# Rotary scores on one core: rows of k laid out like q, whole-batch loads, rotation in place, column order restored by ScalarE

## The chip, the cores and the metric

The kernel runs on one core of one Trainium2 chip. The metric is the device time in microseconds (us). The kernel before takes 808.53 us, the median of three runs (807.85 to 809.18). Everything is fp32.

## The reference

```python
batch, seq, heads, dim = 16, 512, 16, 64
q1, q2 = q[..., :half_dim], q[..., half_dim:]
q_rot = np.concatenate([q1 * cos_q - q2 * sin_q,
                        q1 * sin_q + q2 * cos_q], axis=-1)
# k_rot: the same with k
scores = np.einsum('bshd,bthd->bsht', q_rot, k_rot)
```

Here q and k are [batch, seq, heads, dim], 33.5 MB each, cos and sin are [seq, dim/2], and the scores are [batch, seq, heads, seq], 268.4 MB. There is no scaling and no softmax. For each batch and head the rotated rows of q are multiplied with all 512 rotated rows of k, over a depth of 64.

## The kernel before, in words

**Tiles.** A batch has 512 rows, cut into C = 4 chunks of 128. For q and for the output, chunk c holds the rows 4p + c, with p the partition (line 43 and line 45, pattern "(p c)"). For k, chunk c holds the rows 128c + p (line 44, pattern "(c p)"). One row of q or k is 16 heads x 64 numbers, 4 KB, so a partition's four rows of q lie side by side in memory and its four rows of k do not. One row of the output is 16 heads x 512 numbers, 32 KB.

**One tile of output.** There are 64 tiles, i = 0 to 63, tile i being chunk i mod 4 of batch i // 4. For each, `scores` (line 162) runs eight steps p = 0 to 7. Each step handles two heads: two matmuls into a PSUM buffer `ps` of two banks (three such buffers), then one ScalarE copy of 128x1024 numbers from `ps` to the staging tile `st` (line 179). After the eighth step SyncE issues one store of 4 MB (line 184). There are three staging buffers. Batch 0 is handled in quarters (units of four heads, lines 79 to 87), with stores of 1 MB (line 182), so that work can start early.

**What feeds it.** `load_pair` (line 91) loads two chunks of q or of k, 1 MB, on SyncE's queue. `rope` (line 102) rotates one chunk by three VectorE instructions: a product with cos into a new tile `rot` (line 128), a product with a signed sin table into `part` (line 131), and a sum with the halves of `part` swapped (line 134). `transposed` (line 140) turns a rotated chunk in two groups of four 128x128 transposes on TensorE, each group into one PSUM bank (two such banks), and names the place in `kT` or `qT` where the bank is copied. For k of batches 1 to 15 that place is 128 neighbouring columns for each pair of heads (lines 158 and 159), so a copy of a bank reads and writes in order.

**Order.** It is written out by hand (`tc.manual_schedule()`); each engine works through its own instructions in the order of the program. In tile i of the main loop (lines 247 to 274) the steps 1 and 3 carry the transposes of q of chunk i + 1, copied by VectorE (line 267), and the steps 5 and 6 carry those of k of chunk i + 4, copied by ScalarE (line 269). VectorE's rotation of q for chunk i + 2 and of k for chunk i + 5 is dealt out between them. At the end of each tile one 1 MB load is issued behind the tile's store: of q in odd tiles, of k in even ones. Three input buffers of 1 MB serve k, two serve q.

**Tables.** cos and sin are loaded twice, once in k's row order (runs of 128 bytes) and once in q's (runs of 512 bytes), on ScalarE's queue (line 53), and a signed sin table is built for each (lines 59 and 60).

Of the kernel before, what the change touches and what calls it, by code (L numbers as in the profile page):

```python
# [10 lines left out]
def kernel(  # L11
# [8 lines left out]
    nc = tc.nc  # L20
# [14 lines left out]
    rot_pool = ctx.enter_context(tc.tile_pool(name="rot", bufs=2))  # L35
# [7 lines left out]
    q_v = q.rearrange("b (p c) h d -> b p c h d", c=C)  # L43
    k_v = k.rearrange("b (c p) h d -> b p c h d", c=C)
# [3 lines left out]
    tabs = {}  # L48

    def load_tables(which, pat):  # L50
        for name, src in (("cos", cos), ("sin", sin)):
            t = const_pool.tile([P, C, HD], fp32, name=f"{name}_{which}")
            nc.scalar.dma_start(t, src.rearrange(pat, c=C))
            tabs[name, which] = t

    def build_table(which):

        ss = const_pool.tile([P, C, 2, HD], fp32, name=f"ss_{which}")
        nc.scalar.copy(out=ss[:, :, 0, :], in_=tabs["sin", which])
        nc.scalar.mul(ss[:, :, 1, :], tabs["sin", which], -1.0)  # L60
        tabs["ss", which] = ss.rearrange("p c x j -> p c (x j)")

    in_tiles = {}
    IN_BUFS = {"k": 3, "q": 2}

    def in_tile(which, pair):
        t = in_pool.tile(
            [P, 2, H * D], fp32, tag=which + "_in", bufs=IN_BUFS[which], name=which + "_sb"
        )
        in_tiles[which, pair] = t  # L70
        return t
# [5 lines left out]
    units = {}  # L77

    def load_units(which, head, heads):
        n = C * heads * D  # L80
        t = early[:, load_units.used : load_units.used + n]
        load_units.used += n
        t = t.rearrange("p (c e) -> p c e", c=C)
        src = (k_v if which == "k" else q_v)[0, :, :, head : head + heads, :]
        nc.sync.dma_start(t.rearrange("p c (h d) -> p c h d", d=D), src)
        for h in range(0, heads, G):
            units[which, (head + h) // G] = t[:, :, D * h : D * (h + G)]

    load_units.used = 0

    def load_pair(which, pair):

        b, x = divmod(pair, C // 2)
        if b >= B:
            return
        t = in_tile(which, pair)
        src = (k_v if which == "k" else q_v)[b, :, 2 * x : 2 * x + 2]
        nc.sync.dma_start(t.rearrange("p c (h d) -> p c h d", h=H), src)

    rots = {}  # L100

    def rope(which, n):


        a = rot_pool.tile([P, H * D], fp32, tag="rot_" + which, name=which + "_rot")
        bt = rot_pool.tile([P, H * D], fp32, tag="part", name="part")
        cs, ss = tabs["cos", which], tabs["ss", which]
        if n < C:
            src = units[which, n]
            sv = "p c (g j) -> p c g j"  # L110
            v1 = "p (c g j) -> p c g j"
            k1 = {"c": C, "j": HD}
            cs = cs.unsqueeze(2).to_broadcast((P, C, 2 * G, HD))
            ss = ss.unsqueeze(2).to_broadcast((P, C, G, D))
            k2 = {"c": C, "j": D}
        else:
            src = in_tiles[which, n // 2][:, n % 2]
            sv = "p (g j) -> p g j"
            v1 = "p (g j) -> p g j"
            k1 = {"j": HD}  # L120
            cs = cs[:, n % C].unsqueeze(1).to_broadcast((P, 2 * H, HD))
            ss = ss[:, n % C].unsqueeze(1).to_broadcast((P, H, D))
            k2 = {"j": D}
        swapped = bass.AP(bt.tensor, bt.offset + HD, [bt.ap[0], (D, H), (-HD, 2), (1, HD)])
        a4 = a.rearrange("p (h x j) -> p h x j", x=2, j=HD)
        rots[which, n] = a
        return [
            lambda: nc.vector.tensor_tensor(  # L128
                a.rearrange(v1, **k1), src.rearrange(sv, j=HD), cs, op=mult
            ),  # L130
            lambda: nc.vector.tensor_tensor(  # L131
                bt.rearrange(v1, **k2), src.rearrange(sv, j=D), ss, op=mult
            ),
            lambda: nc.vector.tensor_tensor(a4, a4, swapped, op=add),  # L134
        ]
# [4 lines left out]
    def transposed(which, n, g):  # L140

        rot = rots[which, n]
        bank = ps_t_pool.tile([P, 4, P], fp32, tag="ps_t", name="bank")
        for x in range(4):
            if n < C:
                src = rot.rearrange("p (c e) -> p c e", c=C)[:, x, P * g : P * (g + 1)]
            else:
                src = rot[:, P * (4 * g + x) : P * (4 * g + x + 1)]
            nc.tensor.transpose(bank[:, x, :], src, ident)  # L149
        if which == "q":  # L150
            if n not in qT:
                qT[n] = qt_pool.tile([P, HP, P], fp32, tag="qT", name="qT_t")
            dst = qT[n][:, 4 * g : 4 * g + 4, :]
        else:
            b = n // C
            if b not in kT:
                kT[b] = kt_pool.tile([P, HP, S], fp32, tag="kT", name="kT_t")
            t = kT[b].rearrange("p h (c t) -> p h c t", c=C)
            dst = t[:, 2 * n + g] if n < C else t[:, 4 * g : 4 * g + 4, n % C]
        return bank, dst  # L160

    def scores(i, p, st):

        ps = ps_s_pool.tile([P, 2, S], fp32, tag="ps_s", name="ps")
        b = i // C
        if b == 0:
            c, hp = divmod(p, 2)
            lhs, rhs = qT[i][:, C * hp + c], kT[0][:, 2 * i + hp]
        else:
            lhs, rhs = qT[i][:, p], kT[b][:, p]  # L170
        for r in range(2):
            nc.tensor.matmul(  # L172
                out=ps[:, r, :],
                lhsT=lhs[64 * r : 64 * r + 64, :],
                rhs=rhs[64 * r : 64 * r + 64, :],
                start=True,
                stop=True,
            )
        nc.scalar.copy(out=st[:, 2 * p : 2 * p + 2, :], in_=ps)  # L179
        if b == 0 and p % 2 == 1:  # L180
            c = p // 2
            nc.sync.dma_start(o_v[0, c, :, G * i : G * (i + 1)], st[:, G * c : G * (c + 1)])
        elif b > 0 and p == HP - 1:
            nc.sync.dma_start(o_v[b, i % C], st)

    def tr_act(which, n):
        for g in range(2):
            bank, dst = transposed(which, n, g)
            nc.scalar.copy(out=dst, in_=bank)  # L189

    def run(ops):
        for op in ops:
            op()

    with tc.manual_schedule():
        load_tables("k", "(c p) j -> p c j")
        load_tables("q", "(p c) j -> p c j")
# [3 lines left out]
        load_pair("k", 2)  # L201
        load_pair("q", 2)
        load_pair("k", 3)
        make_identity(nc, ident)
        build_table("k")
        build_table("q")
        run(rope("k", 0))
        tr_act("k", 0)
        run(rope("q", 0))
        tr_act("q", 0)  # L210


        for i in range(C):
            st = st_first[i] if i < 2 else stage_pool.tile([P, H, S], fp32, tag="stage", name="st")
            late = []
            if i > 0:
                late = [("k", C + i - 1, 0), ("k", C + i - 1, 1)]
# [6 lines left out]
            for p in range(HP):  # L224
                scores(i, p, st)
                if p in (0, 1) and late:
                    bank, dst = transposed(*late.pop(0))
                    dve.pop(0)()
                    nc.vector.tensor_copy(out=dst, in_=bank)  # L229
                if i == 0 and p == 1:  # L230
                    load_pair("k", 4)
                if i == 0 and p == 3:
                    load_pair("q", 3)
                if p in (2, 6):
                    m = len(dve) - (6 if p == 2 else 3) + (-3 if i == C - 1 else 0)
                    run(dve[:m])
                    dve = dve[m:]
                    tr_act(*nxt.pop(0))
            run(dve)
            if i == 1:  # L240
                load_pair("k", 5)
            elif i == 3:
                load_pair("q", 4)
                load_pair("k", 6)


        for i in range(C, NST):
# [11 lines left out]
            for p in range(HP):  # L259
                scores(i, p, st)  # L260
                if p not in tr:
                    continue
                bank, dst = transposed(*tr[p])
                if tr[p][0] == "q":
                    run(dve[:1])
                    dve = dve[1:]
                    nc.vector.tensor_copy(out=dst, in_=bank)  # L267
                else:
                    nc.scalar.copy(out=dst, in_=bank)  # L269
            run(dve)  # L270
            if i % 2 == 1:
                load_pair("q", (i + 1) // 2 + 2)
            else:
                load_pair("k", (i + 4) // 2 + 3)
# [30 lines left out]
```

## Time and profile before

| What | Value |
|---|---|
| time, median of three runs | 808.53 us |
| the profiled execution's own time | 811.69 us |
| its span (first to last event in the profile) | 809.9 us |
| busy in the span: TensorE, ScalarE, VectorE | 689.5, 561.8, 522.6 us |
| read from and written to memory by DMA | 67.37 MB and 268.44 MB |
| granted TensorE clock, mean | 0.937 |
| first and last issue of a 4 MB store (line 184) | 71.5 and 787.4 us |

The profile lists, for each engine, how long its instructions were busy, and for each group of instructions (line, operation, tiles, shape) the count, the total and the mean of one. The row of DMA digits is the share of the core's 16 DMA engines that were busy, in 40 slices of the span. A DMA is cut into packets, one for each contiguous run of memory; the trace holds the start, the duration and the size of every packet. "Idle before" is the time in which an engine waited ahead of a group, with what released it.

### The profile page before, as it was taken

To read this page: it belongs to the slowest core of one execution; us is meant where nothing else is said; L and a number is where in the kernel's file an instruction comes from. 1 tells how busy PE (TensorE), PEld (TensorE's weight loads), DVE (VectorE), ACT (ScalarE), POOL (GpSimd) and SP (SyncE) were. 2 spreads that over 40 slices of the span, in tenths; PEclk is the share of its full clock that TensorE was granted. 3 is DMA by queue.
4 is the path that set the end of the run, shared out by engine and by line. 5 is a ranking of instruction groups with operands and counts; after the bars stand their busy time and mean duration, and the time that the engine had idled before them with its cause. 6 is when DMAs were issued, how large, how long until landed. Compare 5 with 4: busy or idle time off the path is not lost.

```text
span 809.9 us, 7719 instructions
## 1 busy us (share of the span) xinstructions
PE 689.5 (85%) x3072; PEld 295.6 (36%) x3072; DVE 522.6 (65%) x508; ACT 561.8 (69%) x649; POOL 0.7 (0%) x6
## 2 busy tenths in 40 slices
PE   4989998898888888888879799797988989889870
PEld 3444443343333333333334333343333333333320
DVE  7899786655767656756568575576755856565400
ACT  4888886676767776767767668676767666777670
POOL 0000000000000000000000000000000000000000
PEclk9999999989999999999999999998989899999895
DMA  9999999999999999999999999999999999999995
GB/s 346 424 424 441 410 420 435 431 419 439 433 420 437 430 423 436 431 424 438 430 422 436 431 424 438 425 429 437 387 431 398 426 410 430 388 367 392 412 415 222
DMA packets 26916, 336.31 MB, mean 415 GB/s; under 512 B 3328, under 2 KB 4608, under 8 KB 13312
## 3 DMA queue, kind: packets, MB, share of 16 engines
q1 hardware_dynamic: 25536, 335.55, 98.2%
q8 instruction: 24, 0.39, 0.2%
q10 hardware_dynamic: 1344, 0.26, 0.2%
q14 instruction: 12, 0.10, 0.0%
HBM read 67.37 MB, written 268.44 MB: 415 GB/s over the span
## 4 chain that ended last, share of the span: by engine, by line
DMA 61%; PE 27%; ACT 6%; DVE 2%; issue 1%; ACTq 0%
DMA out_dram<-st 61%; PE ps L172 20%; PE bank L149 7%; ACT st L179 6%; DVE part L131 1%; DMA cos_k<-in_cos_dram 1%; DVE kT_t L229 0%; DVE q_rot L134 0%; DVE k_rot L134 0%; DVE k_rot L128 0%; DVE q_rot L128 0%; ACTq L300 0%; ACTq L179 0%
## 5 line engine op out<-in xcount | busy, mean ns | idle before, releaser
L179 ACT COPY st<-ps 128x1024 f32<-128x1024 f32 x512 | 494.8, 1019 | 213.5 <-DMA out_dram<-st 145.1
L172 PE MATMUL ps<-kT_t,qT_t 64*128 64x512 f32 x2048 | 546.5, 647 | 82.6 <-ACT st L179 82.6
L172 PEld LDWEIGHTS ps<-kT_t,qT_t 64*128 64x128 f32 x2048 | 180.7, 195 | 277.8 <-ACT st L179 145.5
L128 DVE TENSOR_TENSOR q_rot<-q_sb,cos_q 128x1024 f32<-128x1024 f32 x60 | 73.3, 1221 | 163.4 <-DMA q_sb<-in_q_dram 163.4
L267 DVE COPY qT_t<-bank 128x512 f32<-128x512 f32 x118 | 80.9, 686 | 78.9 <-PE bank L149 78.7
L149 PEld LDWEIGHTS bank<-ident,q_rot 128*128 128x128 f32 x512 | 60.3, 154 | 106.8 <-issue 85.6
L149 PE MATMUL bank<-ident,q_rot 128*128 128x128 f32 x512 | 92.8, 311 | 2.6 <-DVE q_rot L134 2.6
L149 PE MATMUL bank<-ident,k_rot 128*128 128x128 f32 x512 | 83.8, 288 | 11.1 <-DVE k_rot L134 10.8
L149 PEld LDWEIGHTS bank<-ident,k_rot 128*128 128x128 f32 x512 | 54.6, 142 | 104.9 <-issue 52.2
L134 DVE TENSOR_TENSOR k_rot<-k_rot,part 128x1024 f32<-128x1024 f32 x64 | 78.3, 1224 | 2.1
L134 DVE TENSOR_TENSOR q_rot<-q_rot,part 128x1024 f32<-128x1024 f32 x64 | 77.8, 1215 | 0.2
L128 DVE TENSOR_TENSOR k_rot<-k_sb,cos_k 128x1024 f32<-128x1024 f32 x60 | 73.1, 1218 | 0.0
L131 DVE TENSOR_TENSOR part<-k_sb,ss_k 128x1024 f32<-128x1024 f32 x60 | 73.0, 1217 | 0.0
L131 DVE TENSOR_TENSOR part<-q_sb,ss_q 128x1024 f32<-128x1024 f32 x60 | 72.9, 1215 | 0.0
L269 ACT COPY kT_t<-bank 128x512 f32<-128x512 f32 x112 | 66.8, 597 | 0.0
L128 DVE TENSOR_TENSOR k_rot<-early,cos_k 128x1024 f32<-128x1024 f32 x4 | 4.9, 1220 | 5.0 <-DMA cos_k<-in_cos_dram 5.0
L189 ACT COPY qT_t<-bank 128x512 f32<-128x512 f32 x10 | 5.6, 616 | 3.0 <-PE bank L149 3.0
L189 ACT COPY kT_t<-bank 128x512 f32<-128x512 f32 x10 | 5.5, 604 | 2.0 <-PE bank L149 2.0
L229 DVE COPY kT_t<-bank 128x512 f32<-128x512 f32 x6 | 4.1, 686 | 2.6 <-PE bank L149 2.6
L128 DVE TENSOR_TENSOR q_rot<-early,cos_q 128x1024 f32<-128x1024 f32 x4 | 4.9, 1217 | 0.0
L131 DVE TENSOR_TENSOR part<-early,ss_q 128x1024 f32<-128x1024 f32 x4 | 4.9, 1216 | 0.0
L131 DVE TENSOR_TENSOR part<-early,ss_k 128x1024 f32<-128x1024 f32 x4 | 4.9, 1215 | 0.0
(11 smaller groups left out, 3.4 us busy)
## 6 DMA issues: line engine op xcount, KB each, us to landing
out_dram<-st SPq DMA_DIRECT2D x60, 4096.0 KB, 27.7
k_sb<-in_k_dram SPq DMA_DIRECT2D x30, 1024.0 KB, 30.2
q_sb<-in_q_dram SPq DMA_DIRECT2D x30, 1024.0 KB, 28.8
out_dram<-st SPq DMA_DIRECT2D x16, 1024.0 KB, 11.3
early<-in_k_dram SPq DMA_DIRECT2D x1, 1536.0 KB, 9.1
early<-in_q_dram SPq DMA_DIRECT2D x1, 1536.0 KB, 12.4
early<-in_k_dram SPq DMA_DIRECT2D x1, 512.0 KB, 4.0
early<-in_q_dram SPq DMA_DIRECT2D x1, 512.0 KB, 5.5
```

Of the source, the lines that this page charges most:

```text
L128: lambda: nc.vector.tensor_tensor(a.rearrange(v1, **k1), src.rearrange(sv, j=HD), cs, op=mult),
L131: lambda: nc.vector.tensor_tensor(bt.rearrange(v1, **k2), src.rearrange(sv, j=D), ss, op=mult),
L134: lambda: nc.vector.tensor_tensor(a4, a4, swapped, op=add),
L149: nc.tensor.transpose(bank[:, x, :], src, ident)
L172: nc.tensor.matmul(out=ps[:, r, :], lhsT=lhs[64 * r : 64 * r + 64, :], rhs=rhs[64 * r : 64 * r + 64, :], start=True, stop=True,)
L179: nc.scalar.copy(out=st[:, 2 * p : 2 * p + 2, :], in_=ps)
L189: nc.scalar.copy(out=dst, in_=bank)
L229: nc.vector.tensor_copy(out=dst, in_=bank)
L267: nc.vector.tensor_copy(out=dst, in_=bank)
L269: nc.scalar.copy(out=dst, in_=bank)
```

## The change

- k's rows are laid out like q's: partition p holds the rows 4p to 4p + 3 of both. One pair of tables and one signed table serve q and k.
- A load takes a whole batch of q or k, 2 MB, in which each partition reads one run of 16 KB. Before, each load took two chunks, 1 MB, with runs of 8 KB for q and 4 KB for k. There are two buffers of 2 MB each for q and k. In the main loop q of batch b + 2 is issued behind the store of tile 4b + 2 and k of batch b + 3 behind that of tile 4b + 3; the other tiles issue no load.
- The rotation is done in place, in the input tile: the product with sin goes to `part` first (one buffer instead of two), then the input is multiplied by cos in itself, then the sum is made in itself. The tiles `rot` are gone. The transposes read the input tile, which stays occupied until they are done. The two products are one entry of the list that deals out VectorE's work; in batch 0 the sum is two instructions of half the size.
- The columns of `kT` stay in the order (chunk, partition), but column (c, p) now stands for row 4p + c of k. The scores' columns come out in that order, and ScalarE's copy from `ps` to `st` reads PSUM with the innermost step of 128 numbers (four of them, then the next column), which puts the columns back in order. In batch 0 the reordering is done when the bank is copied to `kT`, and the copy of the scores is as before.

```diff
-    k_v = k.rearrange("b (c p) h d -> b p c h d", c=C)
+        "k": k.rearrange("b (p c) h d -> b p c h d", c=C),
...
-    IN_BUFS = {"k": 3, "q": 2}
...
-        t = in_tile(which, pair)
-        src = (k_v if which == "k" else q_v)[b, :, 2 * x : 2 * x + 2]
-        nc.sync.dma_start(t.rearrange("p c (h d) -> p c h d", h=H), src)
+        t = in_pool.tile([P, C, H * D], fp32, tag=which + "_in", name=which + "_sb")
+        batches[which, b] = t
+        nc.sync.dma_start(t.rearrange("p c (h d) -> p c h d", h=H), dram[which][b])
...
+            x4 = x.rearrange("p (h x j) -> p h x j", x=2, j=HD)
+            swapped = bass.AP(part.tensor, part.offset + HD, [part.ap[0], (D, H), (-HD, 2), (1, HD)])
+            adds = [(x4, swapped)]
...
+        def products():
+            nc.vector.tensor_tensor(pv, xs, ss, op=mult)
+            nc.vector.tensor_tensor(xc, xc, cs, op=mult)
+
+        def sums():
+            for y, z in adds:
+                nc.vector.tensor_tensor(y, y, z, op=add)
...
-            t = kT[b].rearrange("p h (c t) -> p h c t", c=C)
-            dst = t[:, 2 * n + g] if n < C else t[:, 4 * g : 4 * g + 4, n % C]
-        return bank, dst
+            if n < C:
+                dst = kT[b][:, 2 * n + g].rearrange("p (t c) -> p t c", c=C)
+                src = bank.rearrange("p c t -> p t c")
+            else:
+                dst = kT[b][:, 4 * g : 4 * g + 4, P * (n % C) : P * (n % C + 1)]
+        copy(out=dst, in_=src)
...
-        nc.scalar.copy(out=st[:, 2 * p : 2 * p + 2, :], in_=ps)
+        so, si = st[:, 2 * p : 2 * p + 2, :], ps
+        if b > 0:
+            so = so.rearrange("s r (t c) -> s r t c", c=C)
+            si = si.rearrange("s r (c t) -> s r t c", c=C)
+        nc.scalar.copy(out=so, in_=si)
...
-        load_tables("k", "(c p) j -> p c j")
-        load_tables("q", "(p c) j -> p c j")
+        for t, src in ((cos_t, cos), (sin_t, sin)):
+            nc.scalar.dma_start(t, src.rearrange("(p c) j -> p c j", c=C))
...
-        load_pair("k", 2)
-        load_pair("q", 2)
-        load_pair("k", 3)
+        load("k", 1)
+        load("q", 1)
...
-                if i == 0 and p == 1:
-                    load_pair("k", 4)
-                if i == 0 and p == 3:
-                    load_pair("q", 3)
+                if p == 3 and i < 2:
+                    load("kq"[i], 2)
...
-            if i == 1:
-                load_pair("k", 5)
-            elif i == 3:
-                load_pair("q", 4)
-                load_pair("k", 6)
+        load("k", 3)
...
-            if i % 2 == 1:
-                load_pair("q", (i + 1) // 2 + 2)
-            else:
-                load_pair("k", (i + 4) // 2 + 3)
+            if i % C == C - 2:
+                load("q", i // C + 2)
+            elif i % C == C - 1:
+                load("k", i // C + 3)
```

More of the change, by code (lines that the diff above doesn't have):

```diff
@@ L34 @@
     in_pool = ctx.enter_context(tc.tile_pool(name="in", bufs=2))
-    rot_pool = ctx.enter_context(tc.tile_pool(name="rot", bufs=2))
+    part_pool = ctx.enter_context(tc.tile_pool(name="part", bufs=1))
     kt_pool = ctx.enter_context(tc.tile_pool(name="kt", bufs=2))
@@ L40 @@
     ps_t_pool = ctx.enter_context(tc.psum_pool(name="ps_t", bufs=2))
-    q_v = q.rearrange("b (p c) h d -> b p c h d", c=C)
-    k_v = k.rearrange("b (c p) h d -> b p c h d", c=C)
+    dram = {
+        "q": q.rearrange("b (p c) h d -> b p c h d", c=C),
+        "k": k.rearrange("b (p c) h d -> b p c h d", c=C),
+    }
     o_v = out.rearrange("b (p c) h t -> b c p h t", c=C)
     ident = const_pool.tile([P, P], fp32, name="ident")
[L48 to L63, printed above, removed]
-    IN_BUFS = {"k": 3, "q": 2}
[L66 to L71, printed above, removed]
+    cos_t = const_pool.tile([P, C, HD], fp32, name="cos_t")
+    sin_t = const_pool.tile([P, C, HD], fp32, name="sin_t")
+    ss_t = const_pool.tile([P, C, 2, HD], fp32, name="ss_t")
+    ss_v = ss_t.rearrange("p c x j -> p c (x j)")
     st_first = [stage_pool.tile([P, H, S], fp32, tag="stage", name="st") for _ in range(2)]
@@ L77 @@
     units = {}
+    used = [0]
     def load_units(which, head, heads):
         n = C * heads * D
[L81 to L84, printed above, removed]
+        t = early[:, used[0] : used[0] + n].rearrange("p (c e) -> p c e", c=C)
+        used[0] += n
+        src = dram[which][0, :, :, head : head + heads, :]
         nc.sync.dma_start(t.rearrange("p c (h d) -> p c h d", d=D), src)
@@ L87, in load_units, with load @@
             units[which, (head + h) // G] = t[:, :, D * h : D * (h + G)]
-    load_units.used = 0
-    def load_pair(which, pair):
-        b, x = divmod(pair, C // 2)
+    batches = {}
+    def load(which, b):
         if b >= B:
             return
-        t = in_tile(which, pair)
-        src = (k_v if which == "k" else q_v)[b, :, 2 * x : 2 * x + 2]
-        nc.sync.dma_start(t.rearrange("p c (h d) -> p c h d", h=H), src)
-    rots = {}
+        t = in_pool.tile([P, C, H * D], fp32, tag=which + "_in", name=which + "_sb")
+        batches[which, b] = t
+        nc.sync.dma_start(t.rearrange("p c (h d) -> p c h d", h=H), dram[which][b])
@@ L102, in rope @@
     def rope(which, n):
-        a = rot_pool.tile([P, H * D], fp32, tag="rot_" + which, name=which + "_rot")
-        bt = rot_pool.tile([P, H * D], fp32, tag="part", name="part")
-        cs, ss = tabs["cos", which], tabs["ss", which]
+        part = part_pool.tile([P, H * D], fp32, tag="part", name="part")
         if n < C:
[L109 to L115, printed above, removed]
-        else:
[L117 to L135, printed above, removed]
+            x = units[which, n]
@@ new lines, in rope @@
+            sv, k1, k2 = "p c (g j) -> p c g j", {"j": HD}, {"j": D}
+            cs = cos_t.unsqueeze(2).to_broadcast((P, C, 2 * G, HD))
+            ss = ss_v.unsqueeze(2).to_broadcast((P, C, G, D))
+            pv = part.rearrange("p (c g j) -> p c g j", c=C, j=D)
+            x5 = x.rearrange("p c (h x j) -> p c h x j", x=2, j=HD)
+            p5 = part.rearrange("p (c h x j) -> p c h x j", c=C, x=2, j=HD)
+            adds = [(x5[:, :, :, y], p5[:, :, :, 1 - y]) for y in range(2)]
+        else:
+            x = batches[which, n // C][:, n % C]
+            sv, k1, k2 = "p (g j) -> p g j", {"j": HD}, {"j": D}
+            cs = cos_t[:, n % C].unsqueeze(1).to_broadcast((P, 2 * H, HD))
+            ss = ss_v[:, n % C].unsqueeze(1).to_broadcast((P, H, D))
+            pv = part.rearrange(sv, **k2)
+            x4 = x.rearrange("p (h x j) -> p h x j", x=2, j=HD)
+            swapped = bass.AP(part.tensor, part.offset + HD, [part.ap[0], (D, H), (-HD, 2), (1, HD)])
+            adds = [(x4, swapped)]
@@ L137, with transposed @@
+        xs, xc = x.rearrange(sv, **k2), x.rearrange(sv, **k1)
+        def products():
[4 more added lines that the diff above has]
+                nc.vector.tensor_tensor(y, y, z, op=add)
+        return [products, sums]
     kT = {}
     qT = {}
-    def transposed(which, n, g):
-        rot = rots[which, n]
+    def transposed(which, n, g, copy):
         bank = ps_t_pool.tile([P, 4, P], fp32, tag="ps_t", name="bank")
@@ L145, in transposed @@
             if n < C:
-                src = rot.rearrange("p (c e) -> p c e", c=C)[:, x, P * g : P * (g + 1)]
+                src = units[which, n][:, x, P * g : P * (g + 1)]
             else:
-                src = rot[:, P * (4 * g + x) : P * (4 * g + x + 1)]
+                src = batches[which, n // C][:, n % C, P * (4 * g + x) : P * (4 * g + x + 1)]
             nc.tensor.transpose(bank[:, x, :], src, ident)
+        src = bank
         if which == "q":
@@ L171, in scores @@
         for r in range(2):
+            po, rh = ps[:, r, :], rhs[64 * r : 64 * r + 64, :]
             nc.tensor.matmul(
[L173 to L177, printed above, removed]
-            )
-        nc.scalar.copy(out=st[:, 2 * p : 2 * p + 2, :], in_=ps)
+                out=po, lhsT=lhs[64 * r : 64 * r + 64, :], rhs=rh, start=True, stop=True
+            )
+        so, si = st[:, 2 * p : 2 * p + 2, :], ps
[3 more added lines that the diff above has]
+        nc.scalar.copy(out=so, in_=si)
         if b == 0 and p % 2 == 1:
@@ L187, in tr_act @@
         for g in range(2):
-            bank, dst = transposed(which, n, g)
-            nc.scalar.copy(out=dst, in_=bank)
+            transposed(which, n, g, nc.scalar.copy)
     def run(ops):
@@ L200 @@
             load_units("q", head, heads)
-        load_pair("k", 2)
-        load_pair("q", 2)
-        load_pair("k", 3)
+        load("k", 1)
+        load("q", 1)
         make_identity(nc, ident)
[L205 to L210, printed above, removed]
+        nc.scalar.copy(out=ss_t[:, :, 0, :], in_=sin_t)
+        nc.scalar.mul(ss_t[:, :, 1, :], sin_t, -1.0)
+        for which in ("k", "q"):
+            run(rope(which, 0))
+            tr_act(which, 0)
         for i in range(C):
             st = st_first[i] if i < 2 else stage_pool.tile([P, H, S], fp32, tag="stage", name="st")
-            late = []
-            if i > 0:
-                late = [("k", C + i - 1, 0), ("k", C + i - 1, 1)]
             if i < C - 1:
@@ L225 @@
                 scores(i, p, st)
[L226 to L229, printed above, removed]
-                if i == 0 and p == 1:
-                    load_pair("k", 4)
-                if i == 0 and p == 3:
-                    load_pair("q", 3)
+                if p in (0, 1) and i > 0:
+                    run(dve[:1])
+                    dve = dve[1:]
+                    transposed("k", C + i - 1, p, nc.vector.tensor_copy)
+                if p == 3 and i < 2:
+                    load("kq"[i], 2)
                 if p in (2, 6):
-                    m = len(dve) - (6 if p == 2 else 3) + (-3 if i == C - 1 else 0)
+                    m = len(dve) - (4 if p == 2 else 2) - (2 if i == C - 1 else 0)
                     run(dve[:m])
@@ L262 @@
                     continue
-                bank, dst = transposed(*tr[p])
                 if tr[p][0] == "q":
@@ L266 @@
                     dve = dve[1:]
-                    nc.vector.tensor_copy(out=dst, in_=bank)
+                    transposed(*tr[p], nc.vector.tensor_copy)
                 else:
-                    nc.scalar.copy(out=dst, in_=bank)
+                    transposed(*tr[p], nc.scalar.copy)
             run(dve)
-            if i % 2 == 1:
-                load_pair("q", (i + 1) // 2 + 2)
-            else:
-                load_pair("k", (i + 4) // 2 + 3)
+            if i % C == C - 2:
+                load("q", i // C + 2)
+            elif i % C == C - 1:
+                load("k", i // C + 3)
 _INS = ['q', 'k', 'cos', 'sin']
```

## The prediction

> **What bounds the kernel now.** I read the page's busy times first, then its DMA rows, then the groups of instructions and the waits, and at last the end of the span in the DMA view.
>
> ```profile
> PE 689.5 (85%) x3072; PEld 295.6 (36%) x3072; DVE 522.6 (65%) x508; ACT 561.8 (69%) x649; POOL 0.7 (0%) x6
> ...
> DMA  9999999999999999999999999999999999999995
> ...
> DMA packets 26916, 336.31 MB, mean 415 GB/s; under 512 B 3328, under 2 KB 4608, under 8 KB 13312
> ...
> q1 hardware_dynamic: 25536, 335.55, 98.2%
> q8 instruction: 24, 0.39, 0.2%
> q10 hardware_dynamic: 1344, 0.26, 0.2%
> ...
> L179 ACT COPY st<-ps 128x1024 f32<-128x1024 f32 x512 | 494.8, 1019 | 213.5 <-DMA out_dram<-st 145.1
> ...
> L267 DVE COPY qT_t<-bank 128x512 f32<-128x512 f32 x118 | 80.9, 686 | 78.9 <-PE bank L149 78.7
> ...
> L269 ACT COPY kT_t<-bank 128x512 f32<-128x512 f32 x112 | 66.8, 597 | 0.0
> ...
> out_dram<-st SPq DMA_DIRECT2D x60, 4096.0 KB, 27.7
> k_sb<-in_k_dram SPq DMA_DIRECT2D x30, 1024.0 KB, 30.2
> q_sb<-in_q_dram SPq DMA_DIRECT2D x30, 1024.0 KB, 28.8
> ```
>
> No compute engine is full, while SyncE's queue (q1) keeps 16 DMA engines busy for 98.2% of the span, and ScalarE's copies wait for a staging buffer, that is for a store (145.1 us). A store takes 27.7 us from issue to landing though its own packets need some 10 us: two tiles of work are always queued ahead of it. So the DMA engines set the time.
>
> The last 12 us say which one (DMA view of 798 to 810 us, 0.3 us to a slice):
>
> ```profile
> DMA  9027902200220002000200020002000200000000
> GB/s 983 0 109 328 1311 0 109 109 0 0 109 109 0 0 0 109 0 0 0 109 0 0 0 109 0 0 0 109 0 0 0 109 0 0 0 0 0 0 0 0
> ```
>
> From about 802 us a single engine works alone, one 32 KB packet every 1.2 us: 15 engines have finished and one is 8.2 us behind. I followed that engine back through the packet records, each packet starting 3 ns before the end of the one ahead. It runs from 4 us to the end with 2.9 us of gaps in all. The others stand idle for 1 to 3 us several times after 700 us, waiting for the next store. So the time is the sum of the packets of the slowest engine.
>
> **The change, part by part.**
>
> *Packets.* Median durations over all engines: 159 ns for 4 KB (k's loads), 309 for 8 KB (q's loads and batch 0's stores), 1213 for 32 KB (stores). A straight line through the last two gives 36.8 ns per 1000 bytes and some 8 ns per packet; 16 KB would take 309 + 8192 x 0.0368 = 610 ns. Less the 3 ns overlap, one engine gives up 480 x 156 = 74.9 us for k and 240 x 306 = 73.4 for q and takes on 240 x 607 = 145.8: a gain of 2.5. On the slow engine the same reads, without their few long packets, average 160 and 311 ns, so 75.4 + 74.0 = 149.4 goes. Its 8 KB reads are 2 to 3 ns above the median, so I take 16 KB at 616 ns: 147.1 comes, a gain of 2.3. The other end is that it slows 16 KB as it does its 32 KB stores (1246 ns instead of 1213): 621 ns, or 148.4, a gain of 1.0. I take 2.3.
>
> *Long packets.* Some reads of that engine take 0.4 to 1.5 us: they cost 4 us in k's 480 packets, 2.7 in q's. If they come by packet, half the packets or fewer leave 3 to 5 us less; if by time or bytes, nothing changes; larger reads could also wait longer, +2. They cluster in time, so I take a gain of only 0.7.
>
> *Fewer DMAs.* 30 loads instead of 60, so 30 completion packets fewer per engine (6 ns each): 0.2. The Trainium skill gives each DMA a fixed cost of about 2 us (page "DMA: Bandwidth & Descriptors", section "Anatomy of one DMA"). By that 30 fewer loads would save 60 us, an estimate. The row of q1 speaks against it: at 98.2% busy that latency lies under other transfers. I count none of it.
>
> *Tables.* k's two tables go: 64 packets of 128 bytes per engine at 13 ns, 0.8 us, in a start with some gaps, so 0.5.
>
> *ScalarE's copy.* The trace has no engine reading at a step; the nearest row is the same copy in order, 1019 ns. With the bank copy (597 ns for half the numbers) that is 0.82 ns per number and 0.17 us fixed. From below, a gain is excluded: the count of numbers is the same. From above I take a doubled slope, 1.86 us. The skill's page "PSUM — Partial Sum Buffer", section "Specifications (TRN2)", speaks against the change: PSUM has lines of 8 bytes, two fp32, and non-contiguous access is said to slow matmuls significantly. With a step of 512 bytes each line serves one number. If ScalarE paid for lines as it now pays for pairs, that is the doubling; but it takes only one number per 0.82 ns, so one line for each may be enough, and the rule is stated for matmuls. I take 1.02 us. ScalarE has room: tiles leave every (787.4 - 71.5)/59 = 12.13 us, and 8 copies with 2 bank copies take 8 x 1.02 + 2 x 0.60 = 9.3. A moderate slowing costs nothing; without that room, each 0.1 us on a copy is 0.8 us a tile, 48 us in all. In batch 0, 8 bank copies on ScalarE read at a step: 5 us in total if doubled, under a queue already filled with loads.
>
> *VectorE.* Six instructions of about 1.22 us and two copies of 0.69 in a tile, before and after: 8.7 of 12.1 us. Taking both products ahead of q's first bank copy delays that copy by 1.2 us at most; behind it stand VectorE's sum and, through the two banks, TensorE's transposes at step 5, and a tile has 3 us to spare. Batch 0's split sums add 8 x about 0.15 us, under the DMA backlog. Nothing on the path.
>
> *Loads.* The q load stands on SP behind the store of tile 4b+2, k's behind 4b+3. Each needs transposes of step 3 or 6 to be done, before the last ScalarE copy that the store itself waits for: no new wait on SP, and nothing but the next store stands behind it. q is needed three tiles later, 36 us; it lands after the backlog, 28.8 us for 1 MB and by rate some 2.5 to 5 us more. If it comes late, VectorE waits a few us; it does now, 163.4 us in 27 waits, at no cost. At the start 8.4 MB instead of 7.3 lie ahead of the first store; at 424 GB/s they last until 22 us and that store is issued at 18 us, so the engines don't run dry. The store backlog of more than 20 us covers the uneven loads later.
>
> Sum: 2.3 + 0.7 + 0.2 + 0.5 = 3.7 us. The profiled execution took 811.69 us, 1.8 outside its span of 809.9, and would take 808.0. The median of the runs is 3.2 us below the profiled one; I take the same 3.7 off it: 808.53 - 3.7 = 804.8 us. What is late next is the same engine.
>
> **The rivals.**
>
> *A, the run length is worth nothing.* Break-even is 149.4/240 = 622.5, so 626 ns per 16 KB packet, 2.5% above the line. For it: the slow engine's 32 KB packets are 2.7% above theirs. Against: its 8 KB reads are not. With no more than the 0.7 of tables and completions left: 807.8. Chance 0.20.
>
> *B, ScalarE becomes the bound.* It happens in the copy from `ps`, for the 60 tiles of batches 1 to 15. It decides from 8x + 1.2 = 12.13, x = 1.37 us a copy, 34% above now. At 1.86 a tile takes 16.1: some 60 us for batch 0, 60 x 16.1 = 966, and the last store of 10: about 1036 us. For it: the step of 512 bytes and the rule above. Against: the copy's pace of one number at a time. Chance 0.06; a further 0.07 that 16 KB reads stall longer on the slow engine (640 ns or more), 811 to 816.
>
> *C, the long packets go with the packets.* Then up to 6.5 instead of 0.7 comes back: 799. For it: they struck reads far more than stores. Against: they cluster. Chance 0.12.
>
> That runs are not 16 KB is unlikely: the stores' runs of 32 KB go as single packets, 7680 of them for 60 tiles x 128.
>
> **How the numbers follow.** The forecast, 2 to 5 us of gain, has 0.55, A 0.20, C 0.12, B with the stalls 0.13. Within 0.2% means 806.9 to 810.1, about what a measurement of this kernel can tell from no change. Faster is the forecast and C: 0.67; same is A: 0.20; slower: 0.13. The range is 799.5 to 809.8; it leaves out B, the stalls and the far end of C.
>
> **What would show it.** Right: 3840 packets of 16 KB near 610 to 616 ns, q1 still near 98%, one engine still last, the copy near 1.02 us and its idle time still with the stores, VectorE's wait for q mostly gone. Wrong: 16 KB packets of 626 ns or more (A), a copy above 1.37 us with ScalarE near full and stores landing in some 12 us instead of 28 (B), or a gap in the DMA row.

## The result, and the profile after

The changed kernel takes 801.01 us (median of 4 runs, 800.67 to 801.41) against 808.79 us of the kernel before: the ratio is 0.9906, with a 95% interval of 0.9888 to 0.9923. It is 7.8 us faster. The forecast was 804.8 us, a gain of 3.7 on the 808.53 us known then. The direction and the bound were right, and the gain was twice what the sum gave.

The page of the changed kernel, with the rows that answer to those shown of before:

```profile
PE 690.9 (86%) x3072; PEld 299.7 (37%) x3072; DVE 544.6 (68%) x516; ACT 561.8 (70%) x647; POOL 0.7 (0%) x6
...
DMA  9999999999999999999999999999999999998995
...
DMA packets 17700, 336.17 MB, mean 421 GB/s; under 512 B 1792, under 2 KB 3072, under 8 KB 4096
...
q1 hardware_dynamic: 17376, 335.55, 98.4%
...
q10 hardware_dynamic: 288, 0.13, 0.1%
...
L162 ACT COPY st<-ps 128x1024 f32<-128x1024 f32 x512 | 495.3, 1018 | 202.8 <-DMA out_dram<-st 113.9
...
L142 DVE COPY qT_t<-bank 128x512 f32<-128x512 f32 x118 | 81.6, 691 | 202.4 <-PE bank L127 202.4
...
L142 ACT COPY kT_t<-bank 128x512 f32<-128x512 f32 x122 | 72.4, 597 | 6.2 <-PE bank L127 6.2
...
out_dram<-st SPq DMA_DIRECT2D x60, 4096.0 KB, 25.0
k_sb<-in_k_dram SPq DMA_DIRECT2D x15, 2048.0 KB, 28.4
q_sb<-in_q_dram SPq DMA_DIRECT2D x15, 2048.0 KB, 27.5
```

The DMA engines are as full as before, with 9,216 packets less on the whole. ScalarE's copy that now reads PSUM at a step takes 1018 ns (1019 before). Its bank copies, eight of which (in batch 0) now also read at a step, take 597 ns on average, as before. VectorE no longer waits for loads of q (163.4 us before); its wait has moved to TensorE's transposes (202.4 us) and costs nothing, since the DMA engines stay full.

The last 12 us, DMA view of 787 to 799 us, slices of 0.3 us:

```profile
DMA  9509950995005200200020002000200020000000
GB/s 546 218 0 874 655 218 0 874 655 218 0 0 219 109 0 0 109 0 0 0 109 0 0 0 109 0 0 0 109 0 0 0 109 0 0 0 0 0 0 0
```

One DMA engine is last again, 7.2 us behind the median of the others (8.2 before). I call it the slow engine and followed it back through the packet records in every kernel below, most of which are introduced in the next section. This table gives its terms in us (a packet counted from its start to the start of the next; "long" is what packets more than a fifth and 20 ns over the median cost; where a kernel ran twice, both profiled executions are shown):

| Kernel | reads, without long | long reads | 4 MB stores | first to last packet | profiled execution |
|---|---|---|---|---|---|
| before | 149.2 | 6.7 | 597.3 | 805.9 | 811.69 |
| changed | 146.6; 146.5 | 2.7; 2.8 | 594.9; 594.6 | 795.0; 794.8 | 800.97; 801.28 |
| 4 KB runs, 2 MB loads | 150.6 | 3.0 | 596.2 | 799.8 | 805.84 |
| 1 MB loads in pairs | 147.7; 147.9 | 3.1; 2.3 | 595.4; 596.2 | 796.6; 798.1 | 803.38; 804.57 |
| 1 MB loads spread | 148.0; 148.0 | 6.8; 4.6 | 596.7; 596.5 | 802.2; 800.6 | 808.52; 807.06 |
| before, loads in pairs | 148.9 | 3.8 | 593.9 | 797.0 | 804.42 |

In all of these the profiled time is the slow engine's span plus 5.8 to 7.4 us. So the time is this engine's sum in each, as the prediction held.

The records do not name the engine of a packet. Where packets of two engines end within a few ns of each other, the path can be followed in more than one way, and the split between long reads and stores is good to 1 or 2 us only. Another way through the same records, which at such places prefers the engine with the longer store packets, gives 6.7 us of long reads again for before, 1.1 to 2.2 for the changed kernel and 2.7 (with stores of 596.1) for "before, loads in pairs"; for the 1 MB loads it gives 2 to 3 in pairs and 4 to 6 spread. Before and the spread loads have the most long reads both ways.

### The profile page after: what moved, and what is told of

It is laid out like the page before. It is cut to its first block, busy times and chain, and to the rows that moved or that the text cites. A ratio compares the mean times of both kernels' runs of the same rounds, so it can differ in the third digit from the quotient of the medians.

```text
span 799.2 us, 7712 instructions
## 1 busy us (share of the span) xinstructions
PE 690.9 (86%) x3072; PEld 299.7 (37%) x3072; DVE 544.6 (68%) x516; ACT 561.8 (70%) x647; POOL 0.7 (0%) x6
## 4 chain that ended last, share of the span: by engine, by line
DMA 50%; PE 37%; DVE 5%; ACT 4%; issue 1%; ACTq 0%; DVEq 0%
DMA out_dram<-st 49%; PE ps L155 28%; PE bank L127 9%; ACT st L162 4%; DVE part L106 2%; DVE early L111 1%; DVE k_sb L107 1%; DVE k_sb L111 1%; DVE early L107 1%; DMA early<-in_k_dram 1%; DVE kT_t L142 0%; DVE q_sb L107 0%; DVE q_sb L111 0%; ACTq L270 0%; DVE qT_t L142 0%
## 5 line engine op out<-in xcount | busy, mean ns | idle before, releaser
L162 ACT COPY st<-ps 128x1024 f32<-128x1024 f32 x512 | 495.3, 1018 | 202.8 <-DMA out_dram<-st 113.9
L142 DVE COPY qT_t<-bank 128x512 f32<-128x512 f32 x118 | 81.6, 691 | 202.4 <-PE bank L127 202.4
L127 PEld LDWEIGHTS bank<-ident,q_sb 128*128 128x128 f32 x480 | 55.6, 152 | 104.5 <-issue 101.9
L127 PE MATMUL bank<-ident,q_sb 128*128 128x128 f32 x480 | 86.8, 309 | 0.9 <-PE ps L155 0.9
L127 PEld LDWEIGHTS bank<-ident,k_sb 128*128 128x128 f32 x480 | 50.5, 141 | 95.1 <-DVE k_sb L107 38.0
L127 PE MATMUL bank<-ident,k_sb 128*128 128x128 f32 x480 | 78.7, 287 | 1.6 <-DVE qT_t L142 1.2
L107 DVE TENSOR_TENSOR q_sb<-q_sb,cos_t 128x1024 f32<-128x1024 f32 x60 | 73.5, 1225 | 2.1
L111 DVE TENSOR_TENSOR k_sb<-k_sb,part 128x1024 f32<-128x1024 f32 x60 | 73.5, 1225 | 2.1
L107 DVE TENSOR_TENSOR k_sb<-k_sb,cos_t 128x1024 f32<-128x1024 f32 x60 | 73.5, 1225 | 2.0
L106 DVE TENSOR_TENSOR part<-q_sb,ss_t 128x1024 f32<-128x1024 f32 x60 | 73.5, 1225 | 2.0
L106 DVE TENSOR_TENSOR part<-k_sb,ss_t 128x1024 f32<-128x1024 f32 x60 | 73.0, 1216 | 0.1
L111 DVE TENSOR_TENSOR q_sb<-q_sb,part 128x1024 f32<-128x1024 f32 x60 | 72.9, 1216 | 0.0
```

The lines of the kernel that those rows point to most:

```text
L106: nc.vector.tensor_tensor(pv, xs, ss, op=mult)
L107: nc.vector.tensor_tensor(xc, xc, cs, op=mult)
L111: nc.vector.tensor_tensor(y, y, z, op=add)
L142: copy(out=dst, in_=src)
L162: nc.scalar.copy(out=so, in_=si)
```

## Experiments

Theories. *Sum*: a packet costs its bytes and some 8 ns, and everything else stays. *Packets*: the long reads come with the number of packets or loads (rival C). *Order*: they come from the order in which stores and loads are issued. Two narrower forms of it come up below: *switches* (the long reads come each time an engine goes from a store to a load) and *restarts* (they come when engines that had run dry start together).

**4 KB runs in loads of 2 MB.** Both patterns changed, order of issues as in the changed kernel:

```diff
-        "q": q.rearrange("b (p c) h d -> b p c h d", c=C),
-        "k": k.rearrange("b (p c) h d -> b p c h d", c=C),
+        "q": q.rearrange("b (c p) h d -> b p c h d", c=C),
+        "k": k.rearrange("b (c p) h d -> b p c h d", c=C),
```

> The changed kernel with q and k both read by the pattern of k before: loads still of 2 MB, but in runs of 4 KB instead of 16 KB. It leaves out the matching of rows: the rows are taken in another order than the tables and the output assume. Theory of the sum (a packet costs its bytes and some 8 ns, all else stays): per engine 960 packets x 157 ns = 150.6 us instead of 240 x 610 = 146.5, so 4.1 us more, 805.1 us. Theory that the long packets come with the number of packets: their cost on the slow engine, 2.7 us in the changed kernel, also goes back to 6.7 or more, so 809 us or more. Theory that the long packets come when the 15 faster engines have run out of work and start together on a new store and load: the order of issues is unchanged, so only the sum, 805.

Measured: 805.4 us (ratio to before 0.9960, 0.9946 to 0.9974), where the theory of packets wanted 809 or more. The reads without long packets are 150.6 us, the number of the sum. The long ones stay at 3.0 us with four times the packets. The theory of packets falls here.

**1 MB loads, in pairs and spread.** In pairs, so that two of every four stores have a pair of loads behind them and the other two have none:

```diff
-        nc.sync.dma_start(t.rearrange("p c (h d) -> p c h d", h=H), dram[which][b])
+        tv = t.rearrange("p c (h d) -> p c h d", h=H)
+        for x in range(2):
+            nc.sync.dma_start(tv[:, 2 * x : 2 * x + 2], dram[which][b][:, 2 * x : 2 * x + 2])
```

> The changed kernel with each 2 MB load cut into two of 1 MB (two chunks each, runs of 8 KB), issued one right after the other in the same place. Sum: 480 packets x 308 ns = 147.9 instead of 146.5 us, and 30 more completions at 6 ns: 1.6 us more, 802.6. If the long packets come with the number of loads or packets, 4 us more again, 806.6. If they come from engines that restart together, 802.6.

Spread: the same packets, but the second half of q goes behind the store of tile 4b + 4 and the second half of k behind that of 4b + 5.

```diff
             if i % C == C - 2:
-                load("q", i // C + 2)
+                load("q", i // C + 2, (0,))
             elif i % C == C - 1:
-                load("k", i // C + 3)
+                load("k", i // C + 3, (0,))
+            elif i % C == 0 and i >= 2 * C:
+                load("q", i // C + 1, (1,))
+            elif i % C == 1:
+                load("k", i // C + 2, (1,))
```

> As the kernel with halved loads, but the halves are spread over the tiles, one 1 MB load behind each store, as in the kernel before. Sum: 802.6. If the long packets come with loads or packets: as the halved kernel, 806.6. If they come from engines that restart together behind a store with a load behind it, the order of issues of the kernel before brings them back late in the run: 805 to 806, 2 to 4 us above the halved kernel.

Measured: 803.74 us in pairs (0.9933, 0.9917 to 0.9949) and 807.07 us spread (0.9974, 0.9961 to 0.9987): 3.3 us between two kernels with equal packets and equal loads. That speaks for the order. Both ran again, on one chip with the changed kernel:

> The spread kernel once more, on one chip with its neighbours: changed kernel, 1 MB loads with runs of 8 KB, one behind each store. Against before it has half of k's packets saved, one pair of tables and no other order of issues: 1.4 us less by the sum, and 0.5 for the tables: about 807. If its 807.1 was the chip, another place in the ladder.

> The halved kernel once more, on the same chip: the same packets and loads as the spread one, only issued in pairs. If the order of issues counts, 3 us below the spread kernel again; if not, equal to it.

> The changed kernel once more, on the same chip, as the end of the ladder: by the sum 1.6 us below the halved one (16 KB instead of 8 KB runs, 30 completions fewer), so 801 to 802.5.

Measured on that chip: before 808.96, spread 807.15 (0.9976, 0.9959 to 0.9992), in pairs 804.04 (0.9930, 0.9904 to 0.9955), changed 801.92 us (0.9902, 0.9867 to 0.9936). The steps are 1.8, 3.1 and 2.1 us. The sum had 1.9, nothing and 1.6 for them. The step between spread and pairs is clear of the intervals both times; that from the pairs to the changed kernel is not, for their intervals overlap.

The two orders on SyncE's queue, the first four rows from 300 us on (start, duration, line, transfer, count; a row with x3 spans the time of all three), each with two rows of its page. In pairs:

```profile
300.95 0.34 SPq L169 DMA_DIRECT2D out_dram<-st  x1
301.40 1.29 SPq L81 DMA_DIRECT2D k_sb<-in_k_dram  x2
310.97 25.06 SPq L169 DMA_DIRECT2D out_dram<-st  x3
336.13 1.74 SPq L81 DMA_DIRECT2D q_sb<-in_q_dram  x2
...
q1 hardware_dynamic: 21696, 335.55, 98.5%
...
L164 ACT COPY st<-ps 128x1024 f32<-128x1024 f32 x512 | 494.6, 1019 | 205.8 <-DMA out_dram<-st 116.4
```

Spread:

```profile
307.76 0.33 SPq L171 DMA_DIRECT2D out_dram<-st  x1
308.15 0.68 SPq L83 DMA_DIRECT2D q_sb<-in_q_dram  x1
321.76 0.33 SPq L171 DMA_DIRECT2D out_dram<-st  x1
322.15 0.69 SPq L83 DMA_DIRECT2D k_sb<-in_k_dram  x1
...
q1 hardware_dynamic: 21696, 335.55, 98.1%
...
L166 ACT COPY st<-ps 128x1024 f32<-128x1024 f32 x512 | 494.2, 1020 | 209.9 <-DMA out_dram<-st 148.6
```

The packets are the same 21,696. ScalarE's wait for a staging buffer goes with the order: 116.4 us in pairs and 148.6 spread, beside 145.1 in before and 113.9 in the changed kernel.

**The order alone, in the kernel before.** Its load of k moves one tile later, behind that of q:

```diff
                 load_pair("q", (i + 1) // 2 + 2)
-            else:
-                load_pair("k", (i + 4) // 2 + 3)
+                load_pair("k", (i + 3) // 2 + 3)
```

> The kernel before, with one edit: in the main loop the 1 MB load of k moves one tile later, behind the load of q, so that every second tile issues 2 MB of loads and the others none. Packets, runs, number of loads, tables, tiles and rotation are those of before. If the order of issues brings part of the gain by itself (the halved loads gained 3.3 us when they were put in pairs), 804 to 806. If the gain is the run length and the fewer loads alone, as before: 808.6.

Measured: 804.95 us (0.9947, 0.9929 to 0.9966), 4.0 us below before on the same chip, with 25,536 packets on q1 as before. On the slow engine the reads' plain cost is unchanged (148.9 for 149.2); long reads and stores together fall from 604.0 to 597.7 us. The page shows it late in the run. The GB/s row of before, then rows of this kernel, 40 slices:

```profile
GB/s 346 424 424 441 410 420 435 431 419 439 433 420 437 430 423 436 431 424 438 430 422 436 431 424 438 425 429 437 387 431 398 426 410 430 388 367 392 412 415 222
```

```profile
GB/s 345 425 423 431 399 427 438 431 424 434 419 438 429 435 426 431 423 439 429 433 427 426 428 436 431 429 429 425 432 438 409 423 433 414 415 422 396 422 399 247
...
q1 hardware_dynamic: 25536, 335.55, 98.7%
...
out_dram<-st SPq DMA_DIRECT2D x60, 4096.0 KB, 24.6
```

From slice 29 on the row of before dips to 387, 398, 388 and 367; with loads in pairs it dips less. In before most of the long reads lie there. Of its 244 long reads after 70 us (all engines), 174 came with 13 or more reads in flight at once, that is where nearly all engines had gone from a store to a load together. That doesn't separate the two orders: with loads in pairs it was about the same share, some 150 of 208. Nor are long reads rarer in pairs over all 16 engines: 137 and 222 in the two executions with 1 MB loads in pairs, 188 and 142 with the same loads spread. What falls with the order is the slow engine's part of them.

**Still larger groups.** k's load goes ahead of the store of its tile, so that q and k make 4 MB of loads in a row:

```diff
+                if p == 6 and i % C == C - 1:
+                    load("k", i // C + 3)
...
-            elif i % C == C - 1:
-                load("k", i // C + 3)
```

> The changed kernel with the load of k issued ahead of the store of its tile instead of behind it, as soon as its buffer is free, so that the loads of q and k lie one behind the other on the queue: 4 MB of loads in a row every fourth tile. Packets and loads are the same. If the long packets come with the switches of the engines from stores to loads (14 of them instead of 28), the slow engine has 1.3 us less of them: 799.7 us. If they come from engines that ran dry and restart together, nothing gets less: 801 to 803.

Measured: 802.06 us (0.9917, 0.9881 to 0.9952), like the changed kernel within the intervals and above the 799.7 that the theory of switches gave. In its one traced execution the slow engine had 4.6 us of long reads (2.4 by the other way of following it), not less than in the changed kernel with twice the switches. The number of switches is unlikely to be the cause.

**Half staging tiles,** six of half the size, stored after four steps, with loads as changed and with loads spread. Apart from the number of buffers and the index arithmetic the edit is:

```diff
-        elif b > 0 and p == HP - 1:
-            nc.sync.dma_start(o_v[b, i % C], st)
+        elif b > 0 and p % 4 == 3:
+            x = p // 4
+            nc.sync.dma_start(o_v[b, i % C, :, HP * x : HP * (x + 1)], st[x])
```

> The changed kernel with six staging tiles of half the size instead of three, each stored as soon as its four steps are done: 2 MB stores in runs of 16 KB. A staging buffer comes free and a store is issued earlier, so the faster engines should not run dry. Price by the sum: 960 packets x 608 ns = 583.7 us instead of 580.8 at the medians, 2.9 us more. If long packets come from restarts, their 2.7 us mostly go: 802.2 us. If they come with the switches from stores to loads, they stay: 803.9.

> The kernel with the loads of 1 MB spread over the tiles (807.1 us), with the same half staging tiles. By the sum 2.9 us more. If long packets come from restarts, their 6.8 us fall to 2 or less: 805 us. If they come with the switches from stores to loads, they stay: 810.

Measured: 804.83 us (0.9942, 0.9923 to 0.9960) and 808.94 us (1.0005, 0.9975 to 1.0034). The profiled execution of the second took 805.43 us, below most of its runs (805.4 to 814.8). Its DMA rows:

```profile
DMA  9999999999999999999999999999999999999992
GB/s 349 420 424 421 422 424 425 426 426 431 427 430 428 428 431 429 429 431 428 428 431 427 430 431 428 430 431 429 428 431 428 430 430 429 429 431 429 430 431 116
```

The dips late in the run are gone. This execution is 1.6 and 3.1 us faster than the two profiled ones with whole tiles; the median of the runs is not, and no trace shows one of the slower ones. The last digit shows where the smooth rate went: the other engines, never held up, finish early, and the slow one now ends 12.4 us behind their median. Its long reads were 3.9 us in this execution (6.8 and 4.6 with whole tiles), and with loads as changed 4.3 us (2.7 with whole tiles). Here the ambiguity is largest: the other way of following it gives 1.0 and 1.2 us. Restarts as the cause are neither shown nor refuted.

**Which engine is slow, and relieving it.** Fifteen tiny loads behind the last store:

```diff
+        scr = part_pool.tile([P, H * D], fp32, tag="part", name="scr")
+        for n in range(1, 16):
+            nc.sync.dma_start(scr[:n, HD * n : HD * (n + 1)], cos[:n])
```

> The changed kernel with 15 tiny loads behind the last store, of 1, 2, ... 15 partitions, one run of 128 bytes each, so that the number of these packets on an engine tells which of the 16 it is (by the page on DMA of the Trainium skill a load of n partitions goes to the lowest n engines). Whatever bounds the kernel, the time is about 1 us more. If a fixed engine is the slow one, its packets of 128 bytes come last, all after some 807 us of the record: 0 of them means the sixteenth engine, 8 the eighth.

Measured: 805.69 us, a single run. The packets of the first seven of these loads follow at once on engines that had finished, 0.3 us or less behind. Directly behind its last 32 KB packet the slow engine had three of the seven. That makes it the fifth engine, if a transfer of n partitions goes to the lowest n engines, as the Trainium skill has it (page "DMA: Bandwidth & Descriptors", section "Why a DMA increments its semaphore by 16 and not by 1"); the records, which name no engine, can't show that rule. The eighth load and the rest came only 1.4 us after that engine was done: SyncE had not issued them before, which is most of the extra time. The last store was then cut, so that by the same rule its last 16 partitions go to the first four engines:

```diff
-            nc.sync.dma_start(o_v[b, i % C], st)
+            o = o_v[b, i % C]
+            n = P if i < NST - 1 else 112
+            nc.sync.dma_start(o[:n], st[:n])
+            for x in range(n, P, 4):
+                nc.sync.dma_start(o[x : x + 4], st[x : x + 4])
```

> The changed kernel with only the last store cut: 112 partitions in one DMA (7 packets for each engine instead of 8) and 16 partitions in four DMAs of 4, which go to the first four engines, none of which is the slow one (it came out as the fifth). If the time is the sum of the slow engine's packets, it falls by one packet of 1.24 us, to 799.8, although four other engines get 3 packets more. If all engines or the bytes set it, nothing changes: 801.0 or, with four engines doing more, above.

Measured: 808.78 us (0.9998, 0.9979 to 1.0016), 7 to 8 us slower than the changed kernel. The test failed for a reason of its own, seen in the DMA view of 775 to 807 us (0.8 us to a slice):

```profile
GB/s 492 246 573 410 328 573 82 655 451 164 410 369 82 451 451 82 573 164 328 287 41 123 82 164 205 82 82 123 82 82 41 41 41 0 41 41 0 41 0 0
```

With the store cut in this way its 32 KB packets took up to 6.8 us instead of 1.2: 43 of them were long after 780 us, and none in the changed kernel. Whether the 112 partitions do it or the four small stores beside them was not separated. The question whether the slow engine can be relieved stays open.

## Why the prediction was right, and where its size was wrong

- *Packets* (2.3 us): right. A 16 KB packet took 611 ns at the median, and 613 to 614 on average on the slow engine, long ones aside; the term came to 149.2 - 146.6 = 2.6 us.
- *Fewer DMAs* (0.2): right, 0.87 to 0.67 us on the slow engine. Of the 60 us estimated from the Trainium skill's fixed cost of a DMA nothing was to be seen. The heading of the section cited, "Anatomy of one DMA — SWDGE (gpsimd) path", limits it to DMAs issued by GpSimd; these are issued by SyncE.
- *Tables* (0.5): too high, as far as the start shows. The packets of batch 0's first loads ended 12.6 us after the first of them before and 12.5 after.
- *ScalarE's copy at a step* (nothing): right, 1018 ns. The line rule of the Trainium skill (page "PSUM — Partial Sum Buffer", section "Specifications (TRN2)"), which is stated for matmuls, did not show in ScalarE's reads, so rival B did not come.
- *VectorE* (nothing on the path): right; busy 522.6 to 544.6 us, waits moved.
- *Long packets* (0.7): mis-sized. In the profiled pair they fell by 4.0 us (4.5 to 5.6 by the other way of following the engine). The measured time came near rival C's 799, but C's reason was wrong: the kernel with 4 KB runs had about as few of them as the changed one.
- *Loads*: this is the step that failed. "The store backlog of more than 20 us covers the uneven loads later" gave the new order of issues a price of nothing, and asked only whether an engine would run dry. The order was worth 3.1 us between the spread and the paired loads and 4.0 us in the kernel before. Without it the other steps from before over the spread and the paired loads to the changed kernel are 1.8 + 2.1 = 3.9 us, for which the sum had 3.5.
- *"What is late next is the same engine"*: right. Its stores, which the sum left alone, took 2.4 us less, batch 0's stores 1.4 and gaps 0.3. In the profiled pair that makes 2.6 + 4.0 + 2.4 + 1.4 + 0.3 + 0.2 = 10.9 us, for 10.7 between the two profiled executions. The medians moved by 7.8: the profiled execution before had been 3.2 us above the median of its runs, and such terms differ from one execution to the next (6.8 and 4.6 us of long reads in the spread kernel).
- *Rival A* (run length worth nothing) fell: from 805.4 with 4 KB to 801.0 and 801.9 with 16 KB runs and the same order.
- *The chances*: the gain of 7.8 us lies outside the 2 to 5 that had the chance of 0.55. It lies inside the range of 799.5 to 809.8 because that reached towards rival C, whose mechanism is not the one at work. That part was luck.

What makes a read long is not settled. Shown is that the order of issues changes the time with equal packets and equal loads, in two kernels. That the number of packets does it is refuted, the number of switches is unlikely, and restarts are neither shown nor refuted.

## What to carry to other kernels

Where the DMA row is full, look for the engine that ends last and sum its packets: what the other engines gain or lose does not show in the time. Longer runs were worth some 6 ns here for each packet saved on an engine (805.4 to 801.0 us for 720 packets), and no fixed cost for each load showed. The order of loads and stores on a full queue had a price of its own: it is worth trying loads in pairs, behind fewer of the stores, before touching layouts, since here one moved line gave about half of what the whole change gave (4.0 of 7.8 us).

## What was not expected of the hardware

- One of 16 DMA engines took 1241 to 1246 ns (median) for a 32 KB store packet and the others 1213, in every kernel looked at with stores of 4 MB, but with reads nearly alike (611 to 614 ns for 16 KB).
- That engine's slowness ends with the computing. In the 60 us ahead of ScalarE's last copy from `ps` its 32 KB packets averaged 1237 to 1244 ns, long ones aside, in ten traces of these kernels, and in the 16 or 17 packets behind that copy 1213 to 1215 (in before the copy ended at 787.4 us, and the engine at 808.6). The loads had ended some 40 us earlier in before, so they are not the reason. What makes it slow until then was not tried.
- The last store, cut into one of 112 partitions and four of 4, ran with packets of up to 6.8 us where one of 128 partitions had 1.2.
- SyncE issued seven more small loads behind a store that one engine had not finished, and the eighth only after it had.
